# Where the last recurrence steps and the convolution stand in a hybrid encoder layer on one Trainium2 core

## The chip, the core and the metric

The kernel runs on one core of one Trainium2 chip. A core has a matrix engine (TensorE, PE in the profile, with its weight loads as PEld), a vector engine (VectorE, DVE), an activation engine (ScalarE, ACT), GpSimd (POOL) and SyncE (SP), each with an instruction queue of its own that it works through in order, and DMA engines that move data. The metric is the device time of one execution in microseconds (us), median of several.

## The reference

One layer over 512 tokens of width 1024. `h = rms_norm(x)` is projected into columns for three mixers and their gates:

- pooling mixer: causal window means of 2, 4, 8 and 16 tokens, minus the token, then a linear map;
- RG-LRU: a width-4 causal depthwise convolution, two block-diagonal gates with sigmoids, and a recurrence over the tokens;
- stick-breaking attention with eight heads of 128.

The part that the change touches is the second mixer:

```python
xc = conv_b + conv_w[0] * up[:, 0:S]
for k in range(1, CONV_WIDTH):
    xc = xc + conv_w[k] * up[:, k:k + S]
...
r = sigmoid(xb @ w_rg + b_rg); i = sigmoid(xb @ w_ig + b_ig)
log_a = (-LRU_C * r) * softplus(-lru_lambda)
a = exp(log_a)
b = sqrt(-expm1(2.0 * log_a)) * (i * xc)
h[t] = a[t] * h[t-1] + b[t]          # an associative scan in the reference
```

Each mixer's result goes through a branch projection, is multiplied by `sigmoid(h @ w_gate + b_gate)` and summed; then come an output projection, a residual, a second norm and a SwiGLU feed-forward of width 2816 with its residual.

## The kernel before

Channels lie on the partitions and tokens along the free axis, except in the q, k, v products. Each matrix product is made of three single-pass products of split operands: `x = xh + xl`, and `xh*wh + xh*wl + xl*wh`. A weight tile of 128x1024 is loaded by SP (`raw` or `qw`), ACT copies it to `whi` (L141) and DVE subtracts to get `wlo` (L142): this pair is **a split**. Three buffers hold split weights, so the split for a later half product can start when PE has left the oldest buffer.

The stages in order: gates of the pooling branch; four recurrence chunks of 256 channels (`lru_chunk(0)` to `lru_chunk(3)`), each a product `ps_lru`, and between and behind them the gate products of the recurrence branch (`gate1(0)` to `gate1(3)`, tile `ps_gate`); then v, k and q in this order as seven-product schemes of the Strassen kind (`ps_q`, L831, products "11", "12", "S2", "S1", "S3", "S4", "22"); the gates of the attention branch in the same way (`ps_gy`, `ps_gx`); pooling and attention; the branch, output and feed-forward products.

The steps of one recurrence chunk c are: first tap of the convolution from PSUM (L634), the other three taps (`conv`, L643, twelve instructions), split of the result (`split`, L648 and L649: `xch`, `xcl`), gate products (`gates`, `lg`, L659) with sigmoids on ACT (L663, L664), `tanh` (L668 on DVE, L671 on ACT), `lru_exp` (exponential, L688, then square root, L694), `lru_decay` (L699 on DVE, and for chunks 2 and 3 an Identity on ACT, L703), `lru_input` (L707, L708), `lru_scan` (L714, two of 512 tokens) and `lru_store` (L720 on ACT, L721 on DVE, and two stores that POOL issues, L723).

What sets the order: such steps are put on a list `bg`, and each `tick` between groups of matmuls traces one of them (two while the list is longer than eight). The tracing order is the base priority. A list scheduler then orders each engine's instructions: among those ready in its own model of the run it takes the one earliest in tracing order, and `tc.high_priority(n)` puts instructions n places ahead of where they were traced. Split weights have 200 + 60 places in all; `conv` and `split` of a recurrence chunk have EARLY = 300, and so does L634. `keep_in_program_order(e)` puts an instruction behind the one traced before it on its engine; here this is done to the exponentials of chunks 2 and 3. Once ordered, an engine's instructions run in that order.

`gate_store` (L602, L603) takes a gate product's sigmoid straight from PSUM into a tile `gt` and stores it to memory through POOL. `prepare_t` makes the differences of the normalised input (hT1 to hT4, L558, L559) that the seven-product schemes multiply. `post`, `snap` (L844) and `final` (L848) take v, k and q out of PSUM. Recurrence, gates, snapshots and some more share thirteen buffers of 128x1024 ("b").

Of the kernel before, what the change touches and what calls it, by code (L numbers as in the profile page):

```python
# [11 lines left out]
AF = mybir.ActivationFunctionType  # L12
# [14 lines left out]
EARLY = 300  # L27
# [40 lines left out]
def layer_kernel(ctx: ExitStack, tc: tile.TileContext, x, xt, vecs, w_in, w_qkv7, w_gate7, w_pool, w_rg, w_ig,  # L68
                 w_branch, w_br7, w_out, w_fg, w_fu, w_fd, w_fd7, out):
    nc = tc.nc  # L70
    act = nc.scalar.activation
# [106 lines left out]
    VKQ = (2, 1, 0)  # L178
# [146 lines left out]
    def vcol(name, i=0):  # L325
        o = VOFF[name] + i
        return vt[:, o:o + 1]
# [26 lines left out]
    bg = []  # L354
# [41 lines left out]
    def chan_chunk(key, rhs, nticks=0, pool=None, pair=False):  # L396
        pss = chunk_psum(key, pool, pair)
        for half in range(2):
            half_chunk(pss if type(pss) is list else [pss[:, j, :] for j in range(2)], key, half, rhs,
                       nticks)  # L400
        return pss
# [28 lines left out]
    hn = [(HH[k // 4][:, k % 4, :], HL[k // 4][:, k % 4, :]) for k in range(KT)]  # L430
# [5 lines left out]
    cneg = cst.tile([P, 8], F32, tag="cneg", name="cneg")  # L436


    with ExitStack() as first:
        ap0 = first.enter_context(tc.tile_pool(name="ap0", bufs=1))  # L440
        pools["ap0"] = ap0
        pb = first.enter_context(tc.tile_pool(name="pb", bufs=4, space=PSUM))
# [119 lines left out]
        def prepare_t():  # L562
            return [lambda: diff_h("T1", lambda: hblk(0, 0), 1, lambda: hblk(0, 1)),
                    lambda: diff_h("T2", lambda: halves(BT["T1"]), -1, lambda: hblk(1, 1)),
                    lambda: diff_h("T3", lambda: hblk(1, 1), 1, lambda: hblk(0, 1)),
                    lambda: diff_h("T4", lambda: halves(BT["T2"]), -1, lambda: hblk(1, 0)),
                    lambda: split_t("T2"), lambda: split_t("T1"), lambda: split_t("T3"), lambda: split_t("T4")]
# [26 lines left out]
        def gate_store(br, c, pss, scaled):  # L594
            gt = b4([2, S], f"gt{br}{c}")
            for j in range(2):
                o = two(gt[:, j, :])
                g = in_order(pss[j])
                if not scaled:
                    dve.tensor_tensor(o, g, two(rb), ALU.mult)  # L600
                    g = o
                act(o, g, AF.Sigmoid, bias=vcol("b_gate", 8 * br + 2 * c + j))  # L602
            nc.gpsimd.dma_start(gd[br, c].rearrange("(j p) t -> p j t", p=P), gt)  # L603


        lw = {}
# [21 lines left out]
        def lru_chunk(c):  # L628
            pair = chan_chunk(("lru", c), hn, 1, pb, True)
            u, xc = pair, b4([2, S], f"xc{c}")  # L630

            with tc.high_priority(EARLY):
                for j in range(2):
                    dve.tensor_scalar(two(xc[:, j, :]), in_order(pair[:, j, :]), vcol("conv_w", 24 + 2 * c + j),  # L634
                                      vcol("conv_b", 2 * c + j), ALU.mult, ALU.add)
            st = lru[c] = {"xc": xc}

            def conv():
                for d in range(1, 4):
                    for j in range(2):  # L640
                        x_, u_ = two(xc[:, j, :]), in_order(u[:, j, :])
                        for o, i in ((x_[:, :, d:], u_[:, :, 0:H - d]), (x_[:, 1, 0:d], u_[:, 0, H - d:])):
                            dve.scalar_tensor_tensor(o, i, vcol("conv_w", 8 * (3 - d) + 2 * c + j), o,  # L643
                                                     ALU.mult, ALU.add)

            def split():
                st["h"], st["l"] = b4([2, S], f"xch{c}", "b", F32R), b4([2, S], f"xcl{c}", "b", F32R)
                dve.tensor_copy(st["h"], xc)  # L648
                dve.tensor_tensor(st["l"], xc, st["h"].bitcast(F32), ALU.subtract)  # L649
                st["r"], st["i"] = b4([2, S], f"lr{c}"), b4([2, S], f"li{c}")  # L650


            def gates(j):
                ct = 2 * c + j
                ps = pb.tile([P, 2, S], F32, tag="mm", name=f"lg{c}{j}")
                for n, (w, x_) in enumerate((("h", "h"), ("h", "l"), ("l", "h"))):
                    for n2 in range(2):
                        q = LH[n2]
                        nc.tensor.matmul(ps[:, n2, :], lw[w][q, ct, :], il(st[x_][q, j, :]),  # L659
                                         start=n == 0, stop=n == 2)  # L660
                for n2 in range(2):
                    q, o = LH[n2], LH[1 - n2]
                    act(two(st["r"][q, j, :]), in_order(ps[q, n2, :]), AF.Sigmoid, bias=vcol("b_rg", ct)[q, :])  # L663
                    act(two(st["i"][q, j, :]), in_order(ps[o, n2, :]), AF.Sigmoid, bias=bigx[o, ct:ct + 1])  # L664

            def tanh():
                st["t"] = b4([2, S], f"lt{c}")
                dve.tensor_tensor(st["i"], st["i"], xc, ALU.mult)  # L668
                for j in range(2):
                    ct = 2 * c + j  # L670
                    act(st["t"][:, j, :], st["r"][:, j, :], AF.Tanh, scale=cpos[:, ct:ct + 1])  # L671

            def early(f):
                with tc.high_priority(EARLY):
                    f()

            def both():
                gates(0)
                gates(1)

            return lambda: early(conv), lambda: early(split), both, tanh

        def lru_exp(cs):
            for c in cs:
                for j in range(2):
                    r = lru[c]["r"][:, j, :]
                    ct = 2 * c + j
                    e = act(r, r, AF.Exp, scale=cneg[:, ct:ct + 1])  # L688

                    if c >= 2:  # L690
                        tc.keep_in_program_order(e)
            for c in cs:
                lru[c]["s"] = b4([2, S], f"ls{c}")
                act(lru[c]["s"], lru[c]["t"], AF.Sqrt)  # L694
# [53 lines left out]
        tick(len(bg))  # L748

        def gate1(c):  # L750
            gate_store(1, c, chan_chunk(("gate", 1, c), hn, 1, pb), True)

        def step(*fs):
            bg.append(lambda: [f() for f in fs])

        def of(f, c):
            return lambda: f(c)
# [9 lines left out]
        c3, s3, g3, t3 = lru_chunk(3)  # L769
        step(c3), step(s3), step(of(lru_decay, 1), of(lru_scan, 0)), step(t2, of(lru_input, 1))  # L770
        gate1(1)
        step(of(lru_scan, 1)), step(g3, of(lru_store, 0)), step(t3, of(lru_store, 1)), step(of(lru_exp, (2, 3)))
        gate1(2)
        for f, c in ((lru_decay, 2), (lru_decay, 3), (lru_input, 2)):
            step(of(f, c))
        bg.extend(prepare_t())
        gate1(3)


        def rows(t, i, j):  # L780
# [55 lines left out]
        for t in VKQ:  # L836
            ps = {}
            r = {}


            def snap(key, src):
                r[key] = b4([2, 512], f"r{t}{key[0]}{key[1]}")
                with tc.high_priority(EARLY):
                    act(two(r[key]), in_order(src), AF.Copy, scale=-1.0 if key[0] else 1.0)  # L844

            def final(key, src):
                v = two(r[key])
                dve.tensor_tensor(v, v, in_order(src), ALU.subtract if key[0] else ALU.add)  # L848
                bg.append(lambda t=t, key=key, v=r[key]: post(t, *key, v))

            def bank(nm):
                ps[nm] = pb.tile([P, 2, 512], F32, tag="mm", name=f"ps_q{t}{nm}")
                return ps[nm]

            for nm in ORDER:
                if nm in ("11", "12", "S1", "22"):
                    bank(nm)
                dst = {"S2": "11", "S3": "11", "S4": "S1"}.get(nm, nm)
                tok_product(t, nm, ps[dst], dst == nm)
                if nm == "11":  # L860
                    snap((0, 0), ps["11"])
                elif nm == "12":
                    final((0, 0), ps["12"])
                elif nm == "S2":
                    snap((0, 1), ps["11"])
                elif nm == "S1":
                    snap((1, 1), ps["S1"])
                elif nm == "S3":
                    final((1, 1), ps["11"])
                    snap((1, 0), ps["11"])  # L870
                elif nm == "S4":
                    final((0, 1), ps["S1"])
                else:
                    final((1, 0), ps["22"])
                if (t, nm) == (VKQ[0], "S3"):
                    for f, c in ((lru_input, 3), (lru_scan, 2), (lru_scan, 3), (lru_store, 2), (lru_store, 3)):
                        step(of(f, c))


        def gate_done(cc, j, t, ps):  # L880
# [7 lines left out]
        for cc in range(2):  # L888
# [14 lines left out]
            for nm in ORDER:  # L903
                ps, half, first_, t, ts_, src, ss = plan[nm]
# [315 lines left out]
    with ExitStack() as third:  # L1220
# [42 lines left out]
        for u, nm in BORDER:  # L1263
# [6 lines left out]
            for w in range(2):  # L1270
                o = ps[:, w, half * H:(half + 1) * H]
# [457 lines left out]
```

## Time and profile before

| what | value |
|---|---|
| median of three runs | 874.85 us (873.82 to 877.39) |
| time of the profiled execution | 873.78 us |
| its span, first to last instruction | 872.0 us |
| granted TensorE clock | 1.000 |
| HBM read, written | 132.71 MB, 18.87 MB |

Busy time is given per engine; an engine's idle time matters only where something that ends the run waits for it. In the timeline, a bracket at the end of a row gives the idle time of the engine just before the instruction, and what released it. Instructions on one engine overlap by about 0.1 us, so a row's duration is a little longer than its distance to the next.

### The profile page before, as it was taken

To read this page: it belongs to the slowest core of one execution; us is meant where nothing else is said; L and a number is where in the kernel's file an instruction comes from. 1 tells how busy PE (TensorE), PEld (TensorE's weight loads), DVE (VectorE), ACT (ScalarE), POOL (GpSimd) and SP (SyncE) were. 2 spreads that over 40 slices of the span, in tenths; PEclk is the share of its full clock that TensorE was granted. 3 is DMA by queue.
4 is the path that set the end of the run, shared out by engine and by line. 5 is a ranking of instruction groups with operands and counts; after the bars stand their busy time and mean duration, and the time that the engine had idled before them with its cause. 6 is when DMAs were issued, how large, how long until landed. Compare 5 with 4: busy or idle time off the path is not lost.

```text
span 872.0 us, 14269 instructions
## 1 busy us (share of the span) xinstructions
PE 859.1 (99%) x5563; PEld 789.4 (91%) x5563; DVE 740.8 (85%) x958; ACT 525.4 (60%) x730; POOL 90.8 (10%) x130
## 2 busy tenths in 40 slices
PE   9999989999999999999999999999999999999998
PEld 7888878888899888889889998889999999999998
DVE  7899797998787699977988796699998888899974
ACT  6655989556956555565665545464555555755642
POOL 1110002132423101000001200000000000031200
PEclk9999999999999999999999999999999999999999
DMA  9586346798592786744636965345543343797913
GB/s 335 160 298 198 97 161 177 206 330 259 174 287 73 228 255 198 225 122 147 216 98 165 201 177 169 98 134 157 144 123 97 104 116 105 232 245 202 195 40 121
DMA packets 116643, 154.08 MB, mean 177 GB/s; under 512 B 8160, under 2 KB 90080, under 8 KB 116576
## 3 DMA queue, kind: packets, MB, share of 16 engines
q1 hardware_dynamic: 103904, 107.30, 38.6%
q0 software_dynamic: 12528, 45.62, 21.8%
q8 instruction: 43, 0.70, 0.3%
q10 hardware_dynamic: 144, 0.26, 0.1%
q14 instruction: 24, 0.20, 0.1%
HBM read 132.71 MB, written 18.87 MB: 174 GB/s over the span
## 4 chain that ended last, share of the span: by engine, by line
PE 77%; DVE 11%; ACT 6%; DMA 3%; issue 2%; SPq 0%; ACTq 0%; DVEq 0%
PE ps_y L318 10%; PE ps_x L318 8%; PE ps_q L831 7%; PE ps_dy L1648 6%; PE ps_dx L1648 5%; DVE wlo L142 3%; PE ps_br L309 3%; PE ps_br L310 3%; PE ps_br L311 3%; PE ps_bY L1274 2%; PE ps_gate L734 2%; PE ps_gy L318 2%; PE ps_bX L1274 2%; PE ps_gx L318 2%; ACT whi L141 2%
## 5 line engine op out<-in xcount | busy, mean ns | idle before, releaser
L141 ACT ACTIVATE whi<-raw 128x1024 fp32r<-128x1024 f32 x69 | 72.8, 1055 | 77.4 <-PE ps_out L310 16.2
L142 DVE TENSOR_TENSOR wlo<-raw,whi 128x1024 fp32r<-128x1024 f32 x69 | 84.3, 1222 | 21.8 <-ACT whi L141 21.3
L142 DVE TENSOR_TENSOR wlo<-qw,whi 128x1024 fp32r<-128x1024 f32 x48 | 58.5, 1222 | 18.2 <-ACT whi L141 18.0
L141 ACT ACTIVATE whi<-qw 128x1024 fp32r<-128x1024 f32 x48 | 50.5, 1054 | 28.9 <-PE ps_q L831 14.8
L1439 ACT ACTIVATE wh_S<-w_S 128x1024 fp32r<-128x1024 f32 x36 | 38.1, 1062 | 32.9 <-PE ps_y L318 19.5
L1552 POOL DMA_DIRECT2D dw<-in_w_down_dram x20 | 16.9, 862 | 306.6 <-DMA dw<-in_w_down_dram 264.3
L1440 DVE TENSOR_TENSOR wl_S<-w_S,wh_S 128x1024 fp32r<-128x1024 f32 x36 | 43.8, 1221 | 3.8 <-ACT wh_S L1439 3.8
L1439 ACT ACTIVATE wh<-w 128x1024 fp32r<-128x1024 f32 x27 | 28.6, 1058 | 27.3 <-issue 9.1
L1440 DVE TENSOR_TENSOR wl<-w,wh 128x1024 fp32r<-128x1024 f32 x27 | 33.0, 1221 | 8.4 <-ACT wh L1439 8.4
L1439 ACT ACTIVATE whdS<-dw 128x1024 fp32r<-128x1024 f32 x20 | 21.2, 1060 | 20.9 <-PE ps_dy L1648 10.6
L1440 DVE TENSOR_TENSOR wldS<-dw,whdS 128x1024 fp32r<-128x1024 f32 x20 | 24.3, 1222 | 5.3 <-ACT whdS L1439 5.3
L1090 DVE TENSOR_TENSOR_SCAN E<-K,ahead 128x512 f32<-128x512 f32 (+3 forms) x32 | 25.4, 815 | 3.9 <-ACT K L1086 3.9
L311 PE MATMUL ps_gate<-HH,wlo 128*128 128x512 f32 x64 | 24.4, 381 | 2.2 <-DVE wlo L142 2.2
L309 PE MATMUL ps_br<-yHH,whi 128*128 128x512 f32 x64 | 24.6, 385 | 1.4 <-ACT up L977 1.4
L309 PE MATMUL ps_lru<-HH,whi 128*128 128x512 f32 x64 | 24.6, 384 | 0.0
L309 PE MATMUL ps_br<-yph,whi 128*128 128x512 f32 x64 | 24.5, 383 | 0.0
L309 PE MATMUL ps_pool<-HH,whi 128*128 128x512 f32 x64 | 24.5, 383 | 0.0
L309 PE MATMUL ps_gate<-HH,whi 128*128 128x512 f32 x64 | 24.4, 381 | 0.0
L310 PE MATMUL ps_lru<-HL,whi 128*128 128x512 f32 x64 | 24.3, 379 | 0.0
L311 PE MATMUL ps_lru<-HH,wlo 128*128 128x512 f32 x64 | 24.3, 379 | 0.0
L310 PE MATMUL ps_gate<-HL,whi 128*128 128x512 f32 x64 | 24.3, 379 | 0.0
L310 PE MATMUL ps_pool<-HL,whi 128*128 128x512 f32 x64 | 24.3, 379 | 0.0
(737 smaller groups left out, 3445.1 us busy)
## 6 DMA issues: line engine op xcount, KB each, us to landing
raw<-in_w_in_dram SPq DMA_DIRECT2D x31, 512.0 KB, 5.4
qw<-in_w_qkv_dram SPq DMA_DIRECT2D x24, 512.0 KB, 7.1
dw<-in_w_down_dram POOLq DMA_DIRECT2D x20, 512.0 KB, 8.7
w<-in_w_ffn_gate_dram SPq DMA_DIRECT2D x36, 256.0 KB, 3.5
w<-in_w_ffn_up_dram SPq DMA_DIRECT2D x36, 256.0 KB, 4.2
raw<-in_w_branch_dram SPq DMA_DIRECT2D x16, 512.0 KB, 3.8
qw<-in_w_qkv_dram POOLq DMA_DIRECT2D x12, 512.0 KB, 8.0
qd<-r POOLq DMA_DIRECT2D x12, 512.0 KB, 7.6
```

Of the source, the lines that this page charges most:

```text
L141: act(hi, raw, AF.Copy)
L142: dve.tensor_tensor(lo, raw, hi.bitcast(F32), ALU.subtract)
L309: nc.tensor.matmul(ps, lh, rh, start=start, stop=False, skip_group_check=skip)
L310: nc.tensor.matmul(ps, lh, rl, start=False, stop=False, skip_group_check=skip)
L311: nc.tensor.matmul(ps, ll, rh, start=False, stop=stop, skip_group_check=skip)
L318: nc.tensor.matmul(o, a_[a][:, w, k, :], il2(b_[b][:, k, :]), start=first and n == k == 0, stop=last and n == 2 and k == 3, skip_group_che ...
L831: nc.tensor.matmul(ps[:, a, :], b_[:, k, ts_], il(a_[:, kk, :]), start=first and n == k == 0, stop=n == 2 and k == 3, skip_group_check=True)
L1090: dve.tensor_tensor_scan(E[:, c0:c0 + n][:, ::-1], K[:, c0 + 1:c0 + n + 1][:, ::-1], ahead[:, S - n:][:, ::-1], 0.0, ALU.mult, ALU.add)
L1274: nc.tensor.matmul(o, ah[x_][:, w, k, :], il2(b[k][y_]), start=first_ and n == k == 0, stop=n == 2 and k == 3, skip_group_check=True)
L1439: act(h, src, AF.Copy)
L1440: dve.tensor_tensor(l, src, h.bitcast(F32), ALU.subtract)
L1648: nc.tensor.matmul(o, a_[a][:, w, k0 + k, :], il2(b_[b][:, k, :]), start=first and i == k == 0, stop=last and i == 2 and k == nk - 1, skip ...
```

## The change

Three edits. The convolution's later taps and the split of its result get 240 places of priority and not 300, so they come behind the 260 of the weights' splits. The exponentials of chunks 2 and 3 are traced after `gate1(3)` and ordered on ACT behind its last sigmoid, which `gate_store` now returns. The other steps of chunks 2 and 3 follow directly on the list, in the order decay 2, input 2, decay 3, scan 2, input 3, store 2, scan 3, store 3; before, two decays and one input were listed ahead of `gate1(3)` and the rest after v's product "S3". `prepare_t` is listed ahead of `gate1(3)` and not behind those steps.

```diff
-                act(o, g, AF.Sigmoid, bias=vcol("b_gate", 8 * br + 2 * c + j))
+                last = act(o, g, AF.Sigmoid, bias=vcol("b_gate", 8 * br + 2 * c + j))
             nc.gpsimd.dma_start(gd[br, c].rearrange("(j p) t -> p j t", p=P), gt)
+            return last
...
             def early(f):
-                with tc.high_priority(EARLY):
+                with tc.high_priority(240):
                     f()
...
-                    e = act(r, r, AF.Exp, scale=cneg[:, ct:ct + 1])
-
-                    if c >= 2:
-                        tc.keep_in_program_order(e)
+                    with tc.issue_after(last_gate.ins) if c >= 2 else ExitStack():
+                        act(r, r, AF.Exp, scale=cneg[:, ct:ct + 1])
...
-        step(of(lru_scan, 1)), step(g3, of(lru_store, 0)), step(t3, of(lru_store, 1)), step(of(lru_exp, (2, 3)))
+        step(of(lru_scan, 1)), step(g3, of(lru_store, 0)), step(t3, of(lru_store, 1))
         gate1(2)
-        for f, c in ((lru_decay, 2), (lru_decay, 3), (lru_input, 2)):
+        bg.extend(prepare_t())
+        last_gate = gate1(3)
+        step(of(lru_exp, (2, 3)))
+        for f, c in ((lru_decay, 2), (lru_input, 2), (lru_decay, 3), (lru_scan, 2), (lru_input, 3), (lru_store, 2),
+                     (lru_scan, 3), (lru_store, 3)):
             step(of(f, c))
-        bg.extend(prepare_t())
-        gate1(3)
...
-                if (t, nm) == (VKQ[0], "S3"):
-                    for f, c in ((lru_input, 3), (lru_scan, 2), (lru_scan, 3), (lru_store, 2), (lru_store, 3)):
-                        step(of(f, c))
```

More of the change, by code (lines that the diff above doesn't have):

```diff
@@ L750, in gate1 @@
         def gate1(c):
-            gate_store(1, c, chan_chunk(("gate", 1, c), hn, 1, pb), True)
+            return gate_store(1, c, chan_chunk(("gate", 1, c), hn, 1, pb), True)
         def step(*fs):
```

## Prediction

> **What bounds the kernel now.** I read the page's first part, then the windows by stage, then PE's timeline for every row with a bracket, and last the ACT and DVE timelines around the brackets.
>
> ```profile
> PE 859.1 (99%) x5563; PEld 789.4 (91%) x5563; DVE 740.8 (85%) x958; ACT 525.4 (60%) x730; POOL 90.8 (10%) x130
> ```
> ```profile
> 60.00:105.00 45.00, 45.00 (x223) 37.89 (x222) 43.10 (x66) 30.61 (x39) 1.65 (x2) 1.00 0.55 179
> 105.00:140.00 35.00, 32.79 (x157) 27.89 (x156) 25.92 (x32) 31.82 (x41) 2.95 (x5) 1.00 0.53 179
> 140.00:177.00 37.00, 34.74 (x161) 29.78 (x160) 35.19 (x31) 26.29 (x29) 8.18 (x11) 1.00 0.69 194
> 177.00:213.00 36.00, 36.00 (x168) 31.55 (x167) 30.83 (x33) 23.21 (x29) 10.62 (x10) 1.00 0.97 304
> ```
> ```profile
> 118.02 0.48 PE L311 MATMUL ps_gate<-HH,wlo 128*128 128x512 f32 x1 [2.21 <-DVE wlo L142]
> ...
> 146.73 0.48 PE L831 MATMUL ps_q<-wlo,HH 128*128 128x512 f32 x1 [1.07 <-DVE wlo L142]
> ...
> 163.73 0.48 PE L831 MATMUL ps_q<-wlo,hT3h 128*128 128x512 f32 x1 [1.18 <-DVE wlo L142]
> ...
> 236.74 0.48 PE L831 MATMUL ps_q<-whi,hT3h 128*128 128x512 f32 x1 [0.45 <-ACT r L844]
> ```
>
> PE is busy for 99% of the span, and the change takes no matmul away. A window row gives the length, then busy time of PE, PEld, DVE, ACT and POOL; 105 to 140 us (chunk 3's convolution and the last gates) and 140 to 177 (v's product) are the two stages that the edits reach, and in the second DVE is busy for 35.19 of 37. The only thing to be won is time in which PE waits. In the stages from the recurrence to the end of q there are the four waits above, 2.21 + 1.07 + 1.18 + 0.45 = 4.91 us, 0.56% of the time. That caps the gain; a loss has no such cap.
>
> **First edit: the convolution behind the splits.** The wait of 2.21 us is for a `wlo`:
>
> ```profile
> 109.61 1.04 ACT L141 ACTIVATE whi<-raw 128x1024 fp32r<-128x1024 f32 x1
> ```
> ```profile
> 110.63 1.52 DVE L634 TENSOR_SCALAR xc<-ps_lru,vt 128x512 f32<-128x512 f32 x2
> 112.07 4.77 DVE L643 SCALAR_TENSOR_TENSOR xc<-ps_lru,vt,xc 128x510 f32<-128x510 f32 x12
> 116.75 1.22 DVE L142 TENSOR_TENSOR wlo<-raw,whi 128x1024 fp32r<-128x1024 f32 x1
> ...
> 119.62 1.22 DVE L649 TENSOR_TENSOR xcl<-xc,xch 128x1024 fp32r<-128x1024 f32 x1
> 120.75 1.22 DVE L142 TENSOR_TENSOR wlo<-raw,whi 128x1024 fp32r<-128x1024 f32 x1
> ```
> ```profile
> 122.97 0.48 PE L659 MATMUL lg<-xch,lwh 64*128 64x512 f32 x2
> ```
>
> Its `whi` was done at 110.65, but DVE did 6.1 us of convolution first (110.63 to 116.75) and then the subtraction to 117.97; PE started at 118.02. With 240 against 260 places the twelve taps yield. The first tap (L634) keeps 300 and still goes first, so the subtraction runs from 112.07 to 113.2; PE wants it at 118.02 - 2.21 = 115.81. **The 2.21 us go.** What is late next: the taps and `xcl` come behind up to three subtractions. The sum of DVE's work to 121.97 is the same in either order, so `xcl` ends by 121.97 and not 120.84; PE without the gap reaches `lg` at 122.97 - 2.21 = 120.76 and its `xcl` pair at 120.98. If PE's order is kept, about 1.0 us of the gain is given back; if `lg` moves behind a few gate matmuls, which are ready, nothing is. So 1.2 to 2.2 us; I take 2.2, because the scheduler orders PE by readiness as well. The taps of chunks 0 to 2 are delayed by at most the same two or three subtractions, 2.3 to 3.4 us. PE shows no wait there in 60 to 105 us, and chunk 1 has room between its `xcl` and its gate product:
>
> ```profile
> 79.62 1.23 DVE L649 TENSOR_TENSOR xcl<-xc,xch 128x1024 fp32r<-128x1024 f32 x1
> 80.75 1.23 DVE L559 TENSOR_TENSOR hT4l<-hT,hT4h 128x1024 fp32r<-128x1024 f32 x1
> ```
> ```profile
> 91.21 0.48 PE L659 MATMUL lg<-xch,lwh 64*128 64x512 f32 x2
> ```
>
> That is 10 us. I cost it at 0; without this cover each chunk could cost its 2.3 us. The second row also settles `prepare_t`: the last of its splits ran at 80.75, 60 us ahead of v, whatever its place on the list. Cost 0; if it fell back into v's product, its four pairs would add 4 x 1.2 us to DVE there.
>
> **Second edit: the exponentials behind the last sigmoid.** ACT before:
>
> ```profile
> 133.71 1.28 ACT L688 ACT_TABLE_LOAD   x1
> 135.01 2.56 ACT L688 ACTIVATE lr<-lr,cneg 128x512 f32<-128x512 f32 x4
> 137.47 1.04 ACT L141 ACTIVATE whi<-qw 128x1024 fp32r<-128x1024 f32 x1
> 138.53 1.28 ACT L694 ACT_TABLE_LOAD   x1
> 139.82 2.01 ACT L694 ACTIVATE ls<-lt 128x1024 f32<-128x1024 f32 x2
> 141.85 1.28 ACT L602 ACT_TABLE_LOAD   x1
> 143.15 0.69 ACT L602 ACTIVATE gt<-ps_gate,vt 128x512 f32<-128x512 f32 x1
> 143.74 1.05 ACT L141 ACTIVATE whi<-qw 128x1024 fp32r<-128x1024 f32 x1
> ```
> ```profile
> 140.91 1.23 DVE L699 SCALAR_TENSOR_TENSOR lt<-lr,lt 128x1024 f32<-128x1024 f32 x1 [1.15 <-ACT ls L694]
> ...
> 144.33 1.22 DVE L699 SCALAR_TENSOR_TENSOR lt<-lr,lt 128x1024 f32<-128x1024 f32 x1
> 145.46 1.22 DVE L142 TENSOR_TENSOR wlo<-qw,whi 128x1024 fp32r<-128x1024 f32 x1
> 146.60 1.22 DVE L707 SCALAR_TENSOR_TENSOR ls<-lr,ls 128x1024 f32<-128x1024 f32 x1
> ...
> 160.22 2.34 DVE L714 TENSOR_TENSOR_SCAN li<-lt,ls 128x512 f32<-128x512 f32 x2
> 162.47 1.21 DVE L142 TENSOR_TENSOR wlo<-qw,whi 128x1024 fp32r<-128x1024 f32 x1
> ...
> 178.16 1.22 DVE L721 TENSOR_TENSOR li<-li,yh 128x1024 fp32r<-128x1024 f32 x1
> ```
> ```profile
> 179.35 1.06 ACT L141 ACTIVATE whi<-qw 128x1024 fp32r<-128x1024 f32 x1 [1.53 <-PE ps_q L831]
> 181.94 1.06 ACT L141 ACTIVATE whi<-qw 128x1024 fp32r<-128x1024 f32 x1 [1.53 <-PE ps_q L831]
> ```
>
> The wait at 146.73 ends with the `wlo` of 145.46. Its `whi` could start when PE left the last gate's weights, about 140.2, but ACT was in a square root, a load and a sigmoid until 143.74, and a decay step took DVE to 145.46. After the change ACT does the third gate's two sigmoids as soon as PE has ended that product, and with no load, since the last function of that kind on ACT is the sigmoid of chunk 3's gates, and this `whi` at 140.2 to 141.3; its `wlo` ends near 142.6, three us ahead of PE. **The 1.07 us go.** The three loads stay three: exponential, square root, and a sigmoid load that moves to the first sigmoid of the attention gates, where this row stands among them:
>
> ```profile
> 273.55 1.33 ACT L884 ACTIVATE gy<-gy,vt 128x512 f32<-128x512 f32 x2 [1.15 <-DVE gy L882]
> ```
>
> There 1.28 us of load stand beside an idle ACT (1.15 us ahead of this pair) and three-deep split buffers; I cost it at 0, and 1.28 if that cover fails.
>
> What is added to v's product: two loads, four exponentials and two square roots on ACT, 2 x 1.28 + 2.56 + 2.01 = 7.1 us from about 141. Behind them on ACT queue the `whi` of v, one per 2.59 us (179.35 to 181.94). **The slack of a split** is two half products less its own time: 2 x 2.59 - 1.06 - 1.22 = 2.9 us. A load with one square root (2.34) passes; with one DVE instruction more (1.13, the step from 144.33 to 145.46) it doesn't: 3.47 - 2.9 = 0.6 us of PE. In 141 to 153 DVE is lighter, for the three steps at 140.91 to 147 (two decays and an input) wait for the roots. They come back after about 153: 3 x 1.13 = 3.4 us more in a stretch in which DVE was full, and the second store's subtraction (178.16) was pushed out of v even before. The 36 us after v hold 36.00 - 30.83 = 5.2 us of idle DVE, so it fits if splits go first. But the list is ordered ahead of time and no instruction is broken off: at 160.22 two scans went ahead of a split, and that is the wait of 1.18 us at 163.73. I keep that one and **add one more of its size, +1.18**; the bounds are none, and one for each `wlo` from 153 to 177:
>
> ```profile
> 153.00:177.00 24.00, 11.24 (x10) 1.00 0.76 230
> ```
>
> These are DVE's instructions of L142 alone, ten, of which one began just before 153: nine to be late. The 0.45 us at 236.74, in q, stay.
>
> [...]
>
> The POOL queue: the two `gt` stores move ahead, the first from 145.66, and the recurrence stores shift by some us.
>
> ```profile
> 143.57 0.87 POOL L218 DMA_DIRECT2D qw<-in_w_qkv_dram  x1 [7.61 <-DVE qs L217]
> ...
> 145.66 0.93 POOL L603 DMA_DIRECT2D gd<-gt  x1
> ```
>
> POOL idled 7.61 us ahead of the load that adds v's weights; a store issued before it costs it 0.93 us at most, and the product that needs it is the fifth, over ten us on. Cost 0. SP's loads aren't passed by anything.
>
> **Sum.** 873.78 - 2.21 - 1.07 + 1.18 = 871.7 us. The profiled execution stands 1.07 us under the median of 874.85 and within the runs shown, so I make no correction.
>
> **Rivals.**
>
> *All waits go.* The recurrence steps fit behind the splits, since each now follows in order and none waits in a lump; the 1.18 and 0.45 go as well: 873.78 - 4.91 = 868.9. For it: PE shows no wait in 177 to 213 with DVE 86% busy. Against it: in v DVE is 95% busy. Chance 0.20.
>
> *The convolution doesn't yield.* The taps yield only to splits traced less than 20 places after them, and the first tap keeps 300; then the 2.21 stay: 873.78 - 1.07 + 1.18 = 873.9. Against it: the late `whi` was done before the convolution began. Chance 0.13.
>
> *The compressed recurrence starves v's splits.* Place: ACT from 141 and DVE from 153 to 177. Price: 1.18 us for each split that gets more than 2.9 us of other work ahead of it, that is three DVE instructions, or a load with a root and one DVE instruction. Eight of the nine late splits: 8 x 1.18 - 3.28 = +6.2, 879.9 us; five make +2.6, 876.4, all nine +7.3, 881.1. It decides against the change from three new stalls on. For it: twelve recurrence steps of 1.13 us (two decays, four of input, four scans, two stores), 13.6 us, in 24 us that also hold nine `wlo`, some 10 us, and the adds that take v out of PSUM. Against it: splits have 260 places ahead of everything traced near them. Chance 0.27.
>
> *The forecast*, 871.7, with none to two new stalls 870.5 to 872.9: chance 0.40.
>
> **Chances and range.** 0.5% of 874.85 is 4.4 us, about what a measurement of this kernel can tell from no change: 870.5 and 879.2 are the bounds. Faster: the first rival and a little of the forecast, 0.21. Slower: the upper part of the third rival, eight stalls and more, 0.17. Within: 0.62. The range runs from 868.5 (all waits gone, and 0.1 us each for the four matmuls that take 0.48 after a wait) to 880.0 (eight stalls); a tenth or so lies above it.
>
> **What would show it.** Right: no bracket on PE near 116 and near 146; exponential loads behind a sigmoid at about 141; a sigmoid load at L884; at most two brackets of about 1.2 us between 150 and 180, for `wlo`. Wrong: the `wlo` before the taps still late, a PE wait for `lg` or `xcl` near 121, waits for PSUM or for a snapshot (L844) in v, or a row of waits between 153 and 177. The forecast falls if the new order moves something that I held still: loads of k's weights, or a stage behind 252.

## The result, and the profile after

The change makes the kernel slower: 886.93 us median (885.96 to 888.20, five runs) against 874.85. The ratio on record is 1.0125, with a 95% interval of 1.0111 to 1.0138; the quotient of the two medians is 1.0138, and the five runs of before spread from 873.82 to 877.39. The forecast was 871.7 in a range of 868.5 to 880.0, so it was wrong in sign and outside its range. The profiled execution took 885.99 us, its span is 884.2, 12.2 us longer than before, and its mean granted clock is 0.994.

These are PE's waits from the recurrence to the end of q in the kernel after, from PE's timeline.

```profile
93.76 0.45 PE L309 MATMUL ps_lru<-HH,whi 128*128 128x512 f32 x1 [0.28 <-DVE xc L644]
...
121.82 0.70 PE L660 MATMUL lg<-xch,lwh 64*128 64x512 f32 x4 [0.23 <-DVE xch L649]
...
124.00 0.48 PE L660 MATMUL lg<-xcl,lwh 64*128 64x512 f32 x2 [1.07 <-DVE xcl L650]
...
152.77 0.48 PE L832 MATMUL ps_q2S<-whi,hT1h 128*128 128x512 f32 x1 [1.76 <-ACT whi L141]
...
154.41 0.80 PE L832 MATMUL ps_q2S<-wlo,hT1h 128*128 128x512 f32 x1 [1.15 <-DVE wlo L142]
...
173.83 0.80 PE L832 MATMUL ps_q<-whi,hT3h 128*128 128x512 f32 x1 [7.49 <-ACT r L845]
...
249.10 0.48 PE L832 MATMUL ps_q<-whi,hT3h 128*128 128x512 f32 x1 [0.44 <-ACT r L845]
```

Three of the four waits of before are gone: the 2.21 us near 116, the 1.07 at 146 and the 1.18 at 163. In their place stand 1.58 us in the convolution stage (0.28 + 0.23 + 1.07), 2.91 us near 152 and **one wait of 7.49 us**, for a snapshot (`r`, L845). All seven make 12.42 us against 4.91: 7.5 of the 12.2 us. PE's first matmul of the attention gates starts at 264.74 against 252.39, 12.3 us later, and the span is 12.2 us longer, so nothing is lost behind it.

Where do the other 4.7 us come from? The windows give length, busy time of PE, PEld, DVE, ACT and POOL, then the granted clock, and last the share and rate of the DMA engines.

```profile
150.00:155.00 5.00, 2.09 (x8) 1.25 (x7) 4.14 (x4) 5.00 (x6) 0.00 (x0) 0.91 0.00 0
155.00:160.00 5.00, 5.00 (x19) 4.17 (x18) 3.90 (x4) 2.27 (x3) 0.89 (x1) 0.75 0.32 108
160.00:166.00 6.00, 6.00 (x30) 5.21 (x28) 5.61 (x5) 3.43 (x4) 0.55 (x1) 1.00 0.75 176
166.00:174.00 8.00, 0.51 (x3) 0.17 (x2) 7.99 (x8) 3.25 (x4) 1.96 (x3) 0.82 0.91 240
174.00:178.00 4.00, 4.00 (x10) 3.19 (x11) 0.12 (x1) 0.69 (x1) 1.25 (x2) 0.50 1.09 415
178.00:182.00 4.00, 4.00 (x20) 3.51 (x19) 1.87 (x2) 1.65 (x2) 0.00 (x0) 1.00 0.75 287
```

In 174 to 178 us, behind the 7.49 us of idle PE, the clock is 0.50 and PE, busy all the time, does ten matmuls where 178 to 182 hold twenty. After the long wait ten matmuls came 0.43 us apart and not 0.216, about 2.1 us more; after the waits near 152, where the clock is 0.75 in 155 to 160 us, seven came 0.45 us apart on the mean, about 1.6 us more. Of the 1.0 us left over, 0.7 us lie ahead of everything that the change touches: PE's row L523, at the same place in PE's order in both kernels, starts at 28.96 before and at 29.67 after. The last 0.3 us are not assigned singly; a bracket leaves out the first matmul's own lengthening (0.48 us at 118.02 before, 0.38 for the rows behind it), and there are seven where there were four.

Why did a snapshot come so late? A snapshot is ACT's copy of a half-finished sum out of PSUM, the memory that PE adds into. Before, ACT took the first one and the one behind S2 at these times, the second as soon as PE had ended the product:

```profile
149.61 1.03 ACT L844 ACTIVATE r<-ps_q 128x1024 f32<-128x1024 f32 x1
...
157.18 1.02 ACT L844 ACTIVATE r<-ps_q 128x1024 f32<-128x1024 f32 x1 [1.53 <-PE ps_q L831]
```

This is ACT's timeline around it in the kernel after.

```profile
149.77 1.06 ACT L693 ACTIVATE ls<-lt 128x1024 f32<-128x1024 f32 x1
...
152.62 1.04 ACT L693 ACTIVATE ls<-lt 128x1024 f32<-128x1024 f32 x1
153.57 1.00 ACT L845 ACTIVATE r<-ps_q 128x1024 f32<-128x1024 f32 x1
...
163.90 1.06 ACT L719 ACTIVATE yh<-li 128x1024 fp32r<-128x1024 f32 x1 [0.95 <-DVE li L713]
...
171.81 1.06 ACT L719 ACTIVATE yh<-li 128x1024 fp32r<-128x1024 f32 x1 [4.32 <-DVE li L713]
172.77 1.01 ACT L845 ACTIVATE r<-ps_q 128x1024 f32<-128x1024 f32 x1
173.68 1.02 ACT L845 ACTIVATE r<-ps_q2S 128x1024 f32<-128x1024 f32 x1
```

Product S2 had ended near 161.6, when PE went on to S1. Its snapshot (172.77) stood on ACT right behind `yh` of chunk 3, before which ACT was idle for 4.32 us, until the last scan was done:

```profile
168.31 1.22 DVE L713 TENSOR_TENSOR_SCAN li<-lt,ls 128x512 f32<-128x512 f32 x1
169.44 1.20 DVE L142 TENSOR_TENSOR wlo<-qw,whi 128x1024 fp32r<-128x1024 f32 x1
170.56 1.22 DVE L713 TENSOR_TENSOR_SCAN li<-lt,ls 128x512 f32<-128x512 f32 x1
```

By the program, S3 is added into the same PSUM bank, so PE may not start it until the snapshot has read the bank; its first matmul, at 173.83, is released by that snapshot (7.49 us, `<-ACT r`). So the wait runs: scan on DVE, `yh` on ACT, snapshot on ACT, S3 on PE. The first snapshot stood behind both square roots in the same way (149.77 to 153.57), and PE's order had put the first matmuls of S1 ahead of S2, where they met a split that wasn't ready.

**Theory H.** The snapshots have 300 places of priority and still came after tiles traced before them. The built programs name which of the thirteen "b" buffers each tile gets, and in which order they are first written (the number is the tile's tracing number):

```
before: ... ls2_1242 ls3_1244 gt12_1246 qs20_1255 qs21_1295 gt13_1328 r200_1384 r201_1459 r211_1498 r210_1539 yh2_1578 yh3_1589
after:  ... gt12_1238 qs20_1247 qs21_1284 gt13_1317 ls2_1358 ls3_1360 r200_1386 yh2_1401 yh3_1418 r201_1475 r211_1514 r210_1555
```

In both programs the buffers are handed out in the order in which their first writers were traced (the numbers rise along each line), and the snapshots' 300 places moved none of them forward in it. Before, all four snapshots (`r2..`) stood ahead of `yh2` and `yh3`. The change put `ls2`, `ls3` ahead of the first and `yh2`, `yh3` ahead of the second, and with them the whole of the recurrence. That this order is what holds the snapshots back is still to be shown by the experiments.

**Rivals**: that the late convolution delays everything (C); that there are too few buffers (N); that DVE is too full for the compressed steps, which was the prediction's third rival (D); that the exponentials' move itself costs (E).

### The profile page after: what moved, and what is told of

Same layout as the page of the kernel before. It is cut to its first block, busy times and chain, and to the rows that moved or that the text cites. A ratio compares the mean times of both kernels' runs of the same rounds, so it can differ in the third digit from the quotient of the medians.

```text
span 884.2 us, 14262 instructions
## 1 busy us (share of the span) xinstructions
PE 864.2 (98%) x5563; PEld 793.0 (90%) x5563; DVE 742.1 (84%) x958; ACT 525.7 (59%) x730; POOL 90.1 (10%) x130
## 4 chain that ended last, share of the span: by engine, by line
PE 80%; DVE 10%; ACT 6%; issue 2%; DMA 1%; SPq 0%; ACTq 0%; DVEq 0%
PE ps_y L318 10%; PE ps_x L318 8%; PE ps_q L832 8%; PE ps_dy L1646 6%; PE ps_dx L1646 5%; PE ps_br L309 3%; PE ps_br L310 3%; PE ps_br L311 3%; PE ps_gate L733 2%; PE ps_bY L1272 2%; PE ps_gy L318 2%; DVE wlo L142 2%; PE ps_bX L1272 2%; PE ps_gx L318 2%; PE ps_out L309 1%
## 5 line engine op out<-in xcount | busy, mean ns | idle before, releaser
L311 PE MATMUL ps_br<-yph,wlo 128*128 128x512 f32 x64 | 24.3, 379 | 0.0
L310 PE MATMUL ps_br<-yHL,whi 128*128 128x512 f32 x64 | 24.3, 379 | 0.0
L311 PE MATMUL ps_br<-yHH,wlo 128*128 128x512 f32 x64 | 24.3, 379 | 0.0
```

Source lines behind the costliest of these rows:

```text
L310: nc.tensor.matmul(ps, lh, rl, start=False, stop=False, skip_group_check=skip)
L311: nc.tensor.matmul(ps, ll, rh, start=False, stop=stop, skip_group_check=skip)
```

## The experiments

Each ratio is to runs of the kernel before on the same chip. Four kernels were run together first.

**a1: the first edit alone.**

```diff
             def early(f):
-                with tc.high_priority(EARLY):
+                with tc.high_priority(240):
```

> The kernel before with the first edit alone (convolution taps and split of the result at 240 places). Theory H (the loss comes from the order in which the thirteen shared buffers are handed out, through the steps' new place, so the convolution edit is harmless): the wait of 2.21 us near 116 goes, small waits for xch, xcl and the taps of about 1.6 us in all take its place as in the changed kernel, the rest as before: 873 us beside 873.8 before. Rival C (the convolution edit delays the recurrence, and the waits in v's product follow from that): the wait of 7.5 us in v shows here too, 880 us or more.

Measured: 875.25 us against 876.32, 0.9987 (0.9974 to 1.0000). No long wait: rival C falls. All ten runs of a1 show a granted clock of 1.000 and average 874.9 us; of the nineteen of before six show 1.000 and average 874.8, and thirteen show 0.997 to 0.999 and average 876.6. So at the same clock this edit gains nothing that these runs can tell; its 0.13% goes with the clock, which fell in none of its runs. The waits of the convolution stage are those of the changed kernel, and two in v's product remain.

```profile
121.70 0.70 PE L659 MATMUL lg<-xch,lwh 64*128 64x512 f32 x4 [0.23 <-DVE xch L648]
...
123.88 0.48 PE L659 MATMUL lg<-xcl,lwh 64*128 64x512 f32 x2 [1.06 <-DVE xcl L649]
...
146.28 0.48 PE L831 MATMUL ps_q<-wlo,HH 128*128 128x512 f32 x1 [0.36 <-DVE wlo L142]
...
168.91 0.48 PE L831 MATMUL ps_q2S<-wlo,HH 128*128 128x512 f32 x1 [1.30 <-DVE wlo L142]
```

**a2: the changed kernel with the convolution back at 300.**

```diff
-                with tc.high_priority(240):
+                with tc.high_priority(EARLY):
```

> The changed kernel with the convolution back at 300 places, so the second and third edit alone. Theory H: the waits of v's product stay (1.8 + 1.2 and 7.5 us, and matmuls at half speed behind them), the 2.2 us wait of the convolution comes back in place of 1.6 us: 886.5 us. Rival C: without the late convolution the recurrence keeps up and the long wait shrinks under 2 us: 878 us or less.

Measured: 888.27 against 876.32, 1.0142 (1.0111 to 1.0174). The same 7.49 us, and the 2.21 us are back. The whole loss belongs to the moved steps.

**a3 and a4: the crossed pair.** Each frees two shared buffers, without touching a step, a priority or the tracing order. Pool `mp` has four buffers, whose last users (the differences of the input) are done early.

```diff
a3
-            h, l = b4([2, S], f"yh{c}", "b", F32R), y.bitcast(F32R)
+            h = (mp.tile([P, 2, S], F32R, tag="m", name=f"yh{c}") if c >= 2 else b4([2, S], f"yh{c}", "b", F32R))
+            l = y.bitcast(F32R)
a4
-                lru[c]["s"] = b4([2, S], f"ls{c}")
+                lru[c]["s"] = mp.tile([P, 2, S], F32, tag="m", name=f"ls{c}") if c >= 2 else b4([2, S], f"ls{c}")
```

> The changed kernel, with the tiles yh of chunks 2 and 3 taken from another pool (one whose four buffers are idle then) and not from the thirteen shared ones. Steps, priorities and tracing order are unchanged. Theory H: the shared buffers are handed out in tracing order, so the snapshot after S2 had to come behind yh of chunk 3 on ACT; now it needs not, and the wait of 7.5 us goes with the 2.1 us of slow matmuls behind it, while the 1.8 + 1.2 us near 152 (behind the square roots' tiles) stay: 876 to 877 us. Rival N (too few buffers): two buffers more are free, both waits go: 871 to 873 us. Rival D (DVE is too full in v's product, whatever the buffers): no difference, 886 us.

> The changed kernel, with the square roots' tiles ls of chunks 2 and 3 taken from that other pool; the tiles yh stay with the shared buffers, so the same number of buffers is freed as with yh elsewhere. The square roots can now be issued ahead of the exponentials. Theory H: the first snapshot comes early and the waits of 1.8 + 1.2 us near 152 go, with their 1.5 us of slow matmuls, but the snapshot after S2 is still behind yh of chunk 3, and a wait of 5 to 8 us stays before S3: 880 to 883 us. Rival N: both go, 871 to 873 us. Rival D: no difference, 886 us.

Measured: a3 878.27 against 876.32, 1.0026 (1.0008 to 1.0045), which on 874.85 is 877.1; a4 884.62, 1.0106 (1.0077 to 1.0135), which on 874.85 is 884.1 and lies above the 880 to 883 expected. PE's waits in v's product, first of a3 and then of a4:

```profile
151.90 0.48 PE L833 MATMUL ps_q2S<-whi,hT1h 128*128 128x512 f32 x1 [1.76 <-ACT whi L141]
...
153.54 0.48 PE L833 MATMUL ps_q2S<-wlo,hT1h 128*128 128x512 f32 x1 [1.16 <-DVE wlo L142]
...
164.92 0.48 PE L833 MATMUL ps_q<-wlo,hT3h 128*128 128x512 f32 x1 [0.75 <-DVE wlo L142]
```

```profile
170.92 0.79 PE L832 MATMUL ps_q<-whi,hT3h 128*128 128x512 f32 x1 [10.13 <-ACT r L845]
```

Each takes away the wait of its own tiles and leaves the other's: with `yh` elsewhere the long wait is gone and the pair of waits near 152 stays; with `ls` elsewhere the pair is gone and the long wait stays. It even grew to 10.13 us, beyond the 5 to 8 expected, for PE was ready for S3 at 160.79 and not at 166.34, 5.5 us earlier, and the last scan ended only 2.9 us earlier (168.87 against 171.78). Two buffers more don't help as such (rival N), and the steps as they stand can run without the loss (rival D).

**b1: both elsewhere** (a3's edit and a4's in one).

> The changed kernel with both the tiles yh and the tiles ls of chunks 2 and 3 taken from the other pool: nothing of the recurrence's second half stands ahead of a snapshot in the order of the shared buffers. Theory H: neither the 7.5 us nor the 1.8 + 1.2 us; what is left is 1.6 us around chunk 3's gate product and 0.5 us in q, perhaps one split late by 0.7: 871 to 873 us, at or a little under the kernel before. Rival D (DVE too full for the compressed steps): three or more waits for wlo between 150 and 180, 876 us or more.

Measured: 873.86 against 876.34, 0.9973 (0.9964 to 0.9982). Neither wait is left; in v's product stand three of about 0.2 us. The window of v's product in this kernel:

```profile
140.00:177.00 37.00, 36.58 (x168) 31.11 (x167) 33.17 (x30) 27.13 (x30) 6.96 (x10) 1.00 0.72 212
```

PE is busy for 36.58 of 37 us, against 34.74 before the change. The compressed recurrence does fit behind the splits.

**b2: only the two stores traced late**, behind S3 as before, with all tiles in their own pool.

```diff
-        for f, c in ((lru_decay, 2), (lru_input, 2), (lru_decay, 3), (lru_scan, 2), (lru_input, 3), (lru_store, 2),
-                     (lru_scan, 3), (lru_store, 3)):
+        for f, c in ((lru_decay, 2), (lru_input, 2), (lru_decay, 3), (lru_scan, 2), (lru_input, 3), (lru_scan, 3)):
...
+                if (t, nm) == (VKQ[0], "S3"):
+                    for f, c in ((lru_store, 2), (lru_store, 3)):
+                        step(of(f, c))
```

> The changed kernel with only the two store steps (which make the tiles yh) traced where they were before, behind v's product S3; all tiles in their own pool, the decays, inputs and scans in the new order. Theory H: the snapshot after S2 is handed its buffer ahead of yh, so the 7.5 us go by the tracing order alone; the waits of 1.8 + 1.2 us, behind the square roots' tiles, stay: 876 to 877 us, as with yh elsewhere. Rival D: the scans and inputs are still compressed, so most of the loss stays: 882 us or more.

Measured: 878.57 against 876.34, 1.0028 (1.0015 to 1.0041), the same as a3. The 7.49 us are gone and the pair near 152 stays.

**b3: exponentials and roots traced where they were before**, the other steps in the new order.

```diff
-                    with tc.issue_after(last_gate.ins) if c >= 2 else ExitStack():
-                        act(r, r, AF.Exp, scale=cneg[:, ct:ct + 1])
+                    e = act(r, r, AF.Exp, scale=cneg[:, ct:ct + 1])
+                    if c >= 2:
+                        tc.keep_in_program_order(e)
...
-        step(of(lru_scan, 1)), step(g3, of(lru_store, 0)), step(t3, of(lru_store, 1))
+        step(of(lru_scan, 1)), step(g3, of(lru_store, 0)), step(t3, of(lru_store, 1)), step(of(lru_exp, (2, 3)))
...
-        step(of(lru_exp, (2, 3)))
```

> The changed kernel with the exponentials and square roots traced where they were before, in the third gate's product and pinned there; the other steps in the new order, so yh of both chunks is still traced ahead of the snapshot after S2. Theory H: the first snapshot is early (no 1.8 + 1.2 us near 152), and the snapshot after S2 still follows yh of chunk 3, but the recurrence starts about ten us earlier, so its wait is shorter: 1 to 5 us and not 7.5; 874 to 880 us. Rival E (the loss is the exponentials' move alone): no long wait, 873 us.

Measured: 883.85 against 876.34, 1.0092 (1.0077 to 1.0108). The pair near 152 is gone, as expected, but the long wait is 9.05 us, not 1 to 5. ACT's timeline:

```profile
168.68 1.06 ACT L720 ACTIVATE yh<-li 128x1024 fp32r<-128x1024 f32 x1 [5.88 <-DVE li L714]
169.64 1.01 ACT L845 ACTIVATE r<-ps_q 128x1024 f32<-128x1024 f32 x1
```

`yh` of chunk 3 came at 168.68, only 3.1 us ahead of the changed kernel's 171.81, although the exponentials were early: the recurrence's end is set by DVE, which works on splits and recurrence in turn from 150 us on. PE, without the pair near 152, was ready for S3 4.7 us earlier (161.65 against 166.34), so the wait grew. That part of my working was wrong; that the exponentials' move is the cause (rival E) falls all the same.

**b4: exponentials and convolution as changed, `ls` elsewhere, and of the other steps only two decays and an input directly behind the exponentials, the rest behind S3 as before.**

> The exponentials behind the last sigmoid and the convolution at 240 as changed, the other steps at their old places in the tracing order (stores behind S3), and the square roots' tiles from the other pool. Theory H: no snapshot stands behind a recurrence tile, so 871 to 873 us, at or a little under the kernel before. Rival E (the exponentials' move itself costs, by loads and exponentials ahead of v's splits): waits for whi or wlo of 3 us and more between 140 and 156, 876 us or more.

Measured: 874.59 against 876.34, 0.9977 (0.9968 to 0.9987); the time is above the 871 to 873 expected. PE's waits in v's product are 0.47, 0.18 and 0.40 us, each for a `wlo`, with none near 152. The exponentials stand where the change put them, so rival E falls here too.

**c1: the snapshots elsewhere.** The changed kernel, with one edit from the other side of the line:

```diff
-                r[key] = b4([2, 512], f"r{t}{key[0]}{key[1]}")
+                r[key] = (mp.tile([P, 2, 512], F32, tag="m", name=f"r{t}{key[0]}{key[1]}") if t == VKQ[0]
+                          else b4([2, 512], f"r{t}{key[0]}{key[1]}"))
```

> The changed kernel with all steps, priorities and recurrence tiles as they are; only v's four snapshots are taken from the other pool. This is the other side of the same order: the snapshots no longer stand in the line for the shared buffers at all. Theory H: the long wait goes as it did with yh elsewhere, and the 1.8 + 1.2 us near 152 go too: 871 to 874 us. If the loss came from where yh and ls stand on ACT or from their number, the wait would stay: 880 us or more.

Measured: 873.47 against 875.80, 0.9975 (0.9964 to 0.9985). This is the changed kernel with its recurrence tiles where they were, and it beats both the kernel before and the changed one. All of PE's waits from 60 us to the end of q:

```profile
93.23 0.45 PE L309 MATMUL ps_lru<-HH,whi 128*128 128x512 f32 x1 [0.28 <-DVE xc L644]
...
121.28 0.70 PE L660 MATMUL lg<-xch,lwh 64*128 64x512 f32 x4 [0.22 <-DVE xch L649]
...
123.45 0.48 PE L660 MATMUL lg<-xcl,lwh 64*128 64x512 f32 x2 [1.06 <-DVE xcl L650]
...
167.02 0.48 PE L832 MATMUL ps_q2S<-wlo,HH 128*128 128x512 f32 x1 [0.55 <-DVE wlo L142]
...
180.60 0.48 PE L832 MATMUL ps_q<-wlo,HH 128*128 128x512 f32 x1 [0.23 <-DVE wlo L142]
...
235.97 0.48 PE L832 MATMUL ps_q<-whi,hT3h 128*128 128x512 f32 x1 [0.54 <-ACT r L846]
```

And this is ACT in c1:

```profile
145.64 1.01 ACT L846 ACTIVATE r<-ps_q 128x1024 f32<-128x1024 f32 x1
...
151.07 1.06 ACT L693 ACTIVATE ls<-lt 128x1024 f32<-128x1024 f32 x1
...
155.82 1.00 ACT L846 ACTIVATE r<-ps_q 128x1024 f32<-128x1024 f32 x1
...
162.48 1.06 ACT L719 ACTIVATE yh<-li 128x1024 fp32r<-128x1024 f32 x1 [1.37 <-DVE li L713]
```

The first snapshot now stands ahead of both roots and the one behind S2 ahead of `yh`, with the tracing order and the 300 places of the changed kernel: out of the shared line, priority does move them. That shows theory H from both sides.

**c2: b1 with the convolution back at 300.**

> The kernel with tiles yh and ls elsewhere, and the convolution back at 300 places: what the first edit is worth once the rest is mended. The wait of 2.2 us at the late split comes back, and the 1.6 us around chunk 3's gate product go: 0.6 us slower than with 240 places, 873 to 875 us. If the convolution edit has a hidden cost elsewhere, it is faster.

Measured: 874.56 against 875.80, 0.9990 (0.9976 to 1.0004). Beside b1's 0.9973 the first edit is worth some 1.5 us, within the two intervals' width; its 2.2 us wait is back. Here too it is mostly the clock: the five runs of c2 with a granted clock of 1.000 average 873.7 us and the seven below it 876.0, while b1's nine at 1.000 average 873.6.

## Why the prediction was wrong

- **What bounds the kernel, and the cap on the gain**: right. PE's waits are the whole story, with their slow matmuls.
- **First edit, "the 2.21 us go"**: right. **"So 1.2 to 2.2 us; I take 2.2"**: mis-sized. 0.28 + 0.23 + 1.07 us came in their place, so 0.63 us were won in brackets. In time it was less: from the first `lg` to v's first matmul PE took 63.53 us before and 63.21 after (76.57 to 140.10, 77.28 to 140.49), 0.3 us. That is below the lower bound, because `xcl` was taken to end by 121.97 and ended at 123.94: DVE did chunk 2's product (L669) ahead of it, which I had not counted, and PE's order kept `lg` in place.

```profile
119.86 1.22 DVE L142 TENSOR_TENSOR wlo<-raw,whi 128x1024 fp32r<-128x1024 f32 x1
120.99 0.69 DVE L649 CAST xch<-xc 128x1024 fp32r<-128x1024 f32 x1
121.59 1.22 DVE L669 TENSOR_TENSOR li<-li,xc 128x1024 f32<-128x1024 f32 x1
122.72 1.22 DVE L650 TENSOR_TENSOR xcl<-xc,xch 128x1024 fp32r<-128x1024 f32 x1
```

- **Second edit, "the 1.07 us go"**: right; no wait near 146 in the kernel after. But with the first edit alone (a1) only 0.36 us of it were left, so most of it is not the second edit's.
- **"What is added to v's product", with one new stall of 1.18 us**: the step that failed, and the one that turned the sign. It asked only what is queued behind the new loads and roots, and answered: the splits, which are protected. The snapshots queue there too. I took their 300 places of priority to protect them and didn't ask what else holds a tile back: each needs one of thirteen shared buffers, and those go out in tracing order. In place of +1.18 stand 2.91 + 7.49 us of waits, and some 3.7 us of slow matmuls behind them. I had listed "waits for a snapshot (L844) in v" among the signs of being wrong, but no rival gave it a price.
- **The third rival** (compressed steps starve the splits) gave the right sign for the wrong reason. In b1 and c1 the same steps run in the same stretch and PE loses 0.6 to 0.8 us to late splits there.
- **The sum without the failed step**: c1's ratio of 0.9975 on 874.85 is 872.7 us, 1.0 us above the forecast, and that nearness is in part luck. From L523 (28.96 before, 29.14 in c1) to the first matmul of the attention gates (252.39, 251.62) PE saves 0.95 us, not the 2.1 us of the sum. At a granted clock of 1.000, c1's eleven runs average 873.6 us and the seven such runs of before beside them 874.7; the rest of the ratio comes from the other sixteen runs of before, at 0.997 to 0.999 and 876.3 us, and the sum had no term for the clock. So the waits that the edits were to remove were read rightly, their worth was put too high, and one line of waiting was missed.
- **The table loads**: right at 1.28 us each. Before, the root at 139.82 started 1.29 us after the start of its load at 138.53; after the change the root at 149.77 started 1.30 us after the start of its load, the row that follows. The third load moved to the first sigmoid of the attention gates (L882, 282.32), as forecast.

```profile
148.47 1.28 ACT L693 ACT_TABLE_LOAD   x1
```

What stays open: why a wait of 2.9 us in two pieces slowed the clock in the profiles of the changed kernel and of a2 (granted clock 0.75 and 0.66 in 155 to 160 us) and not in those of b2 (1.00 there) and a3 (1.000 over its whole profiled run; the matmul behind the second piece took 0.80 us in the changed kernel and 0.48 in a3). No run here was made to test it.

## What to carry to other kernels

Before a step is traced earlier, list every tile that it writes and ask which pool each comes from and who is next in line there: priority moves an instruction, but in this kernel it didn't move a tile's turn for a shared buffer. A short tile with a strict deadline (here a snapshot that frees a PSUM bank) should not share buffers with a long chain; four buffers elsewhere turned a loss of 1.25% into a gain of 0.25%, of which some 0.12% stand at the same granted clock. When an urgent instruction is late, look at the instruction just ahead of it on its own engine, and what that one waits for.

## What the runs showed of the hardware

The long waits cost more than their length: behind 7.49, 9.05 and 10.13 us (the changed kernel, b3, a4) the granted clock was 0.50 (in 174 to 178 us of the first, 166 to 174 of the others), the first matmul took 0.79 to 0.80 us, and ten came 0.43 us apart and not 0.216 in the changed kernel. Shorter waits did so in some profiles only: a wait of 2.21 us before was followed by a matmul of 0.48 us and others 0.216 us apart, a2's of 2.21 us by one of 0.48 too, but from 0.8 us on the matmuls came 0.43 us apart (119.06 to 122.04), and c2's of 2.20 us at the same place by one of 0.80. The two kernels whose longest wait is this one of 2.2 us (before and c2) show a granted clock of 1.000 in 24 of 81 runs; the four whose longest wait behind PE's first matmul is 1.4 us (a1, b1, b4, c1) in 42 of 43. Of the two kernels only c2's profile, with a granted clock of 0.998, shows a slow matmul behind this wait, and the one of before, at 1.000, shows none; that the clock fell there in the other runs of these two is inferred from the counts.

```profile
118.50 0.80 PE L311 MATMUL ps_gate<-HH,wlo 128*128 128x512 f32 x1 [2.20 <-DVE wlo L142]
```
